# Side work of the mixers in small jobs let in by weight pieces on a credit, the output projection between queries and values of the next block's first pair, and longer norm gaps

## The chip, the cores and the metric

The kernel runs on one core of a Trainium2 chip. The metric is the device time of one execution in microseconds (us); before the change the median of three runs is 2594.67 us. Five engines work beside each other: PE (matmuls), DVE and ACT (elementwise work), POOL (here little more than clearing buffers) and SP (here the issue of DMAs). Each takes its own instructions in program order, and semaphores make one wait for another.

## The reference

One layer of a decoder trunk for 2048 tokens of width 1024, all in float32: a token mixer with three kinds of heads, then a gated MLP, each behind an RMS norm whose scale and shift come from a conditioning vector.

```python
c_act = jax.nn.silu(c)
mod = (c_act @ w_ada[l] + b_ada[l])[:, None, :]
sh1, sc1, g1, sh2, sc2, g2 = jnp.split(mod, 6, axis=-1)
h = rms_norm(x) * (1.0 + sc1) + sh1
x = x + g1 * token_mixer(h, w_in[l], ...)      # retention | HGRN2 | GLA, one output projection
h = rms_norm(x) * (1.0 + sc2) + sh2
x = x + g2 * conv_ffn(h, w_up[l], conv_w[l], conv_b[l], w_down[l])
return rms_norm(x) * final_gain
```

HGRN2 and GLA are recurrences with a decay for each key channel, `S_t = diag(exp(log_f_t)) S_{t-1} + k_t^T v_t`, `o_t = q_t S_t`, taken in chunks of 64 tokens; retention has a fixed decay for each head.

## The kernel before

Tokens lie along the free axis, in four blocks b = 0 to 3 of 512. A block goes through seven units, `ORDER` = h0, h1, g, h2, h3, r0, r1: four pairs of HGRN2 heads, all GLA heads, two pairs of retention heads. Names in the profile end in block and unit (qbh1_0: block 1, unit h0); the profile's groups leave the numbers out. A full-precision product is three matmuls of 128x512 on halves hi and lo of both factors (`split3`, L232 to L234).

**Weights.** `piece` (L213) and `tf512` (L274) fetch a weight in pieces of 512 KB: SP issues the load of the raw piece (r..., L220 or L282), ACT casts it to hi (h..., L221 or L285), and lo (l...) is computed by DVE in the first block, kept in DRAM, and reloaded from there later (L223, L290). There are two raw buffers and three each of hi and lo.

**A unit.** `unit_h` computes the forget gate (gemm pshf), the queries (pshq), and, for each second unit, the values and gates of the pair (psvg, four pieces in `tf512`). It then hands `gated` to a chain: seven levels, each of them four small matmuls (lv, L607), DVE scaling of queries and keys (L615, L617) and a masked copy (L629); then the keys' transposes (kT), the state update (u; S, L658), the output (o), its head norm (`post`, L542, L543) and, after a gap `POST_GAP`, the transposes to oT (L549, L552, L553). GLA and retention are alike.

**The order.** PE's order is written by hand. A `Clock` adds up the planned time of the matmuls that the projections issue (`adv`) and lets in steps of the chains when their time has come; `at(us, fn)` puts one in later, `until` runs them until a condition holds. The gaps count planned matmul time. The order of DVE, ACT and SP is made by a scheduler from the program order with priorities (`tc.high_priority`).

**Side work**, which no matmul of its own block waits for at once:
- conditioning rows, 48 in all: a load of 512 KB (wada, L190) and one DVE instruction (L197). Rows 16 to 47 run beside the mixers: the list `later` holds their numbers, and each weight piece takes one from it and runs it whole, load and use together.
- norm statistics of the next block (`norm1_stat`, L477): eight loads of x, squares on ACT, sums on DVE (san), then ssn and bcn on PE (`rstd`, L316 and L326) and Newton steps between them.
- the second half of the output projection of block b-1 (`out_finish`, L944): four pieces wo, eight outputs y, the residual (L937), the sums for the second norm (n2), and then `then`: eight rows of the normalised block, stored to h2d (L963 to L965). In block 0's case `then` waits in `put_off` until unit r0 of block 1 has been issued.
- sums of blocks of w_up and w_down for the MLP, in groups (`weight_sums_load` L884, `weight_sums` L892): two loads of 512 KB (wsd, wsu), four DVE additions (L896 to L899), two stores (L902). The main loop loads one or two groups ahead of a unit and sums them behind it. `early_sums` does a like thing with rows of h2d in block 3.

The loads of conditioning rows and sums share four buffers (xy). In the main loop `out_finish(b - 1)` stands behind unit h1 of block b, that is behind the pair's values; `norm1_stat` stands ahead of unit h3:

```python
            if i == len(ORDER) - 3 and b + 1 < NB:
                norm1_stat(b + 1)
...
            mk[kind](b, u, pos)
...
            if i == 1 and b:
                clock.until(lambda: None not in oTs[b - 1])
                out_finish(b - 1)
            for w in ws:
                weight_sums(*w)
```

Behind the mixers (from about 1310 us) the MLP runs; the change doesn't touch it.

Of the kernel before, what the change touches and what calls it, by code (L numbers as in the profile page):

```python
# [3 lines left out]

# [9 lines left out]
AF = mybir.ActivationFunctionType  # L14
# [34 lines left out]

M512, M256, MF = 0.227, 0.12, 0.224  # L50
LEVEL_GAP = (3.2, 4.8)
POST_GAP = 12.0


class Clock:
# [45 lines left out]
def trunk(ctx, tc, xT, vecs, cvec, cst, rope, msk, wada, win, walow, wgla, wout, wup, wdown, out):  # L101
# [91 lines left out]
    def ada(m, raw=None):  # L193

        if raw is None:
            raw = ada_load(m, False)
        V.tensor_tensor_reduce(raw[:], raw[:], c_act[:], 1.0, bada1[:, m:m + 1], op0=ALU.mult, op1=ALU.add,  # L197
                               accum_out=mod[:, m:m + 1])
# [30 lines left out]

    def split3(ps, lhs, rhs, first, last, more=False):  # L230
# [41 lines left out]
    def tf512(name, i, step=2):  # L272

        pss = [acc_ps(f"ps{name}_{c}") for c in range(NCH)]  # L274
        for q4 in range(4):
            half, sub = q4 // 2, q4 % 2
            src = win[i + half:i + half + step + 1:step][:, :, sub * 512:(sub + 1) * 512].rearrange("a p n -> p a n")
            if later:
                ada(later.pop(0))
            with tc.high_priority(offset=50):  # L280
                raw = pw.tile([P, 2, 512], F32, tag="wraw", name=f"r{name}_{q4}", bufs=NRAW)
                nc.sync.dma_start(raw[:], src)  # L282
                hi = pw.tile([P, 2, 512], F32R, tag="whi", name=f"h{name}_{q4}")
                lo = pw.tile([P, 2, 512], F32R, tag="wlo", name=f"l{name}_{q4}")
                S.copy(hi[:], raw[:])  # L285
                key = f"t{i}_{q4}l"
                flat = lo[:].rearrange("p a n -> p (a n)")
                one = [f"i{i + half + step * a}l" for a in range(2)]
                if key in kept:
                    nc.sync.dma_start(flat.bitcast(F32), kept[key][:])  # L290
# [40 lines left out]
    def sumsq(acc, x, k, name, sl=slice(0, TB), first=None):  # L331
        if k == 0 if first is None else first:
            S.activation(acc[:, sl], x[:, sl], AF.Square)
        else:
            sq = late(f"sq{name}{k}")
            S.activation(sq[:, sl], x[:, sl], AF.Square)
            V.tensor_tensor(acc[:, sl], acc[:, sl], sq[:, sl], op=ALU.add)

    def new_acc(name):
        return px.tile([P, TB], F32, tag="ssacc", name="sa" + name, bufs=1)  # L340
# [134 lines left out]
        return W  # L475

    def norm1_stat(b):  # L477
        acc = new_acc(f"n1_{b}")
        for k in range(KD):
            x = tmp(f"x{b}_{k}")  # L480
            nc.sync.dma_start(x[:], xT[b, :, k, :])
            sumsq(acc, x, k, f"n1_{b}_")
        bc1[b] = new_bc1(b)
# [99 lines left out]
    def gated(name, b, ui, pos, kq, decay, subs, qk, sel):  # L583
# [104 lines left out]
    def unit_h(b, u, pos):  # L688
# [122 lines left out]
    def retention(nm, b, r, pos, a, kk, kc, q, vsg):  # L811
# [54 lines left out]
            post(o, sg, nm)  # L866
        adv(12 * MF)
        yield None
        yield POST_GAP
        transposed(b, pos, o, nm)  # L870
        adv(4 * MF)

# [69 lines left out]
    put_off = []  # L942

    def out_finish(b, after_pieces=None, begun=None):  # L944


        acc = new_acc(f"n2_{b}")
        out_half(b, 1, acc, after_pieces, begun)
        rows = list(x1)
        bc = px.tile([P, TB], F32, tag="bc2", name=f"bc2_{b}", bufs=1)  # L950

        for m in range(KD if b == 0 else 0):
            nc.sync.dma_start(x1d[b, m][:], rows[m])

        def then():
            with tc.high_priority(offset=HOT if 0 < b < NB - 1 else -100):
                for m in range(KD):
                    t = rows[m] if b == NB - 1 else tmp(f"t2_{b}_{m}")[:]
                    if b == 0:
                        nc.sync.dma_start(t, x1d[b, m][:])  # L960
                    else:
                        nc.sync.dma_start(x1d[b, m][:], rows[m])
                    V.scalar_tensor_tensor(t, rows[m] if b else t, SC2[:, m:m + 1], bc[:], op0=ALU.mult, op1=ALU.mult)  # L963
                    S.activation(t, t, AF.Identity, bias=SH2[:, m:m + 1])
                    nc.sync.dma_start(h2d[b, m][:], t)  # L965
            done.add(("n2", b))
        clock.at(4.0 if b < NB - 1 else 5.5,
                 rstd(acc, f"n2_{b}", bc[:], then if b else lambda: put_off.append(then), gap=6.5))


    nth = {"w4": 0}
# [90 lines left out]
    gla_weights()  # L1062
    for hi, lo, raw, i in W0.values():
        keep(f"i{i}l", lo[:])
    jobs = [job for k in range(NF // 2) for job in (("d", k), ("u", 2 * k + 1))] + [("u", 0)]
    for b in range(NB):
        pos = 0
        for i, (kind, u) in enumerate(ORDER):
            if i == len(ORDER) - 3 and b + 1 < NB:
                norm1_stat(b + 1)  # L1070
            if b == 0 and i == 2:
                later += range(16, 24)
            if b == 1 and i == 1:
                later += range(24, 40)
            ws, es = [], None
            if b and i >= (3 if b == 1 else 1):
                ws = [weight_sums_load(*jobs.pop(0)) for _ in range(2 if b == 2 or (b, i) == (NB - 1, 5) else 1)]
            if b == NB - 1 and 1 <= i <= 4:
                es = early_sums_load(i - 1)
            mk[kind](b, u, pos)  # L1080
            pos += 2 if kind == "g" else 1
            if b == 1 and i == 5:
                assert not later
                later += range(40, 48)
                clock.until(lambda: put_off)
                put_off.pop()()
            if i == 1 and b:
                clock.until(lambda: None not in oTs[b - 1])
                out_finish(b - 1)
            for w in ws:  # L1090
                weight_sums(*w)
            if es:
                early_sums(*es)
# [481 lines left out]
```

## Time and profile before

| | |
|---|---|
| runs | 2594.67 us median of 3 (2591.9 to 2595.21) |
| profiled execution | 2594.2 us, span 2592.4 us |
| PE busy | 2495.8 us (96%) |
| DVE, ACT, POOL busy | 1993.2 us (77%), 1138.3 us (44%), 160.3 us (6%) |
| mean granted clock of PE | 0.987 |
| chain that ended last | PE 76%, DVE 12%, DMA 6%, issue 3% |

The span is the time from the first to the last instruction. Busy times are sums of an engine's instructions; the chain is followed back from the last instruction to whatever released each one. The mixers' four blocks take the time to about 1310 us; from there to the end the MLP keeps PE busy with little left over (561.58 of the 563 us from 1310 to 1873).

### The profile page before, as it was taken

To read this page: it belongs to the slowest core of one execution; us is meant where nothing else is said; L and a number is where in the kernel's file an instruction comes from. 1 tells how busy PE (TensorE), PEld (TensorE's weight loads), DVE (VectorE), ACT (ScalarE), POOL (GpSimd) and SP (SyncE) were. 2 spreads that over 40 slices of the span, in tenths; PEclk is the share of its full clock that TensorE was granted. 3 is DMA by queue.
4 is the path that set the end of the run, shared out by engine and by line. 5 is a ranking of instruction groups with operands and counts; after the bars stand their busy time and mean duration, and the time that the engine had idled before them with its cause. 6 is when DMAs were issued, how large, how long until landed. Compare 5 with 4: busy or idle time off the path is not lost.

```text
span 2592.4 us, 35722 instructions
## 1 busy us (share of the span) xinstructions
PE 2495.8 (96%) x12418; PEld 2098.8 (81%) x12418; DVE 1993.2 (77%) x3654; ACT 1138.3 (44%) x1946; POOL 160.3 (6%) x287
## 2 busy tenths in 40 slices
PE   5999999999998999999999999999999999999998
PEld 4888887888876888788878888888877888888887
DVE  8877878878677776776788888886777777778666
ACT  3333333334343343433465445555444545455542
POOL 1000000000000000000010000000001100100000
PEclk9999999999999999999999999999999999999999
DMA  8653538866478855787664454478676454447763
GB/s 307 216 160 123 172 121 299 306 200 212 161 262 305 282 165 163 282 291 239 201 212 157 151 168 148 145 226 284 202 240 183 141 158 145 139 150 230 232 193 133
DMA packets 233028, 525.05 MB, mean 203 GB/s; under 512 B 25456, under 2 KB 28560, under 8 KB 232848
## 3 DMA queue, kind: packets, MB, share of 16 engines
q1 hardware_dynamic: 229648, 512.28, 60.0%
q0 software_dynamic: 3200, 10.49, 1.1%
q8 instruction: 98, 1.61, 0.3%
q14 instruction: 82, 0.67, 0.1%
HBM read 397.37 MB, written 125.30 MB: 202 GB/s over the span
## 4 chain that ended last, share of the span: by engine, by line
PE 76%; DVE 12%; DMA 6%; issue 3%; ACT 1%; SPq 0%; DVEq 0%; ACTq 0%; POOL 0%; POOLq 0%
PE X L232 6%; PE X L234 6%; PE X L233 6%; PE Z L233 3%; PE Z L234 3%; PE lvh L607 3%; PE Z L232 3%; PE dX L233 3%; PE dX L232 3%; PE dX L234 3%; PE psvgh L232 2%; PE psvgh L233 2%; PE psvgh L234 2%; PE psqkvgr L232 2%; PE psqkvgr L234 2%
## 5 line engine op out<-in xcount | busy, mean ns | idle before, releaser
L232 PE MATMUL X<-B,A 128*128 128x512 f32 x572 | 224.1, 392 | 1.5 <-ACT u L1282 1.5
L233 PE MATMUL X<-B,A 128*128 128x512 f32 x572 | 223.5, 391 | 0.0
L234 PE MATMUL X<-B,A 128*128 128x512 f32 x572 | 223.3, 390 | 0.0
L998 DVE TENSOR_TENSOR dA<-rd,dA 128x512 fp32r<-128x512 f32 x154 | 106.1, 689 | 89.4 <-ACT dA L997 89.2
L997 ACT CAST dA<-rd 128x512 fp32r<-128x512 f32 x154 | 95.6, 621 | 141.1 <-PE dY L234 43.4
L998 DVE TENSOR_TENSOR A<-s,A 128x512 fp32r<-128x512 f32 x176 | 120.5, 686 | 40.9 <-ACT A L997 40.7
L232 PE MATMUL dX<-dB,dA 128*128 128x512 f32 x352 | 136.9, 389 | 0.0
L233 PE MATMUL dX<-dB,dA 128*128 128x512 f32 x352 | 136.9, 389 | 0.0
L234 PE MATMUL dX<-dB,dA 128*128 128x512 f32 x352 | 136.9, 389 | 0.0
L997 ACT CAST A<-s 128x512 fp32r<-128x512 f32 x176 | 108.7, 618 | 64.2 <-PE Z L234 45.2
L232 PEld LDWEIGHTS X<-B,A 128*128 128x128 f32 x572 | 107.9, 189 | 25.2 <-ACT u L1282 2.8
L234 PEld LDWEIGHTS X<-B,A 128*128 128x128 f32 x572 | 107.9, 189 | 22.4
L233 PEld LDWEIGHTS X<-B,A 128*128 128x128 f32 x572 | 108.0, 189 | 22.4
L607 PEld LDWEIGHTS lvh<-qbh,kh 128*128 128x128 f32 x896 | 116.8, 191 | 11.3 <-issue 3.5
L233 PE MATMUL Z<-B,A 128*128 128x512 f32 x308 | 120.4, 391 | 3.6 <-DVE B L998 3.6
L607 PE MATMUL lvh<-qbh,kh 128*128 128x128 f32 x896 | 120.8, 277 | 2.6 <-DVE kh L617 2.6
L234 PE MATMUL Z<-B,A 128*128 128x512 f32 x308 | 120.1, 390 | 0.0
L232 PE MATMUL Z<-B,A 128*128 128x512 f32 x308 | 119.9, 389 | 0.0
L998 DVE TENSOR_TENSOR dB<-rb,dB 128x512 fp32r<-128x512 f32 x154 | 105.5, 686 | 8.5 <-ACT dB L997 8.5
L998 DVE TENSOR_TENSOR A<-r,A 128x512 fp32r<-128x512 f32 x130 | 89.3, 687 | 28.5 <-ACT A L997 28.5
L232 PE MATMUL psvgh<-hvgh,ha 128*128 128x512 f32 (+1 forms) x256 | 103.1, 403 | 7.0 <-DVE sqh L702 3.7
L232 PE MATMUL psqkvgr<-hqkvgr,ha 128*128 128x512 f32 x256 | 106.2, 415 | 2.4 <-DVE sgh L530 1.7
(461 smaller groups left out, 7015.8 us busy)
## 6 DMA issues: line engine op xcount, KB each, us to landing
gs<-yv SPq DMA_DIRECT2D x154, 256.0 KB, 2.9
rb<-gs SPq DMA_DIRECT2D x154, 256.0 KB, 4.1
r<-wup SPq DMA_DIRECT2D x140, 256.0 KB, 3.5
s<-sumsu SPq DMA_DIRECT2D x136, 256.0 KB, 3.2
wada<-wada SPq DMA_DIRECT2D x48, 512.0 KB, 6.0
rd<-sumsd SPq DMA_DIRECT2D x88, 256.0 KB, 4.1
rd<-wdown SPq DMA_DIRECT2D x66, 256.0 KB, 3.9
x<-xT SPq DMA_DIRECT2D x64, 256.0 KB, 5.4
```

The lines of the kernel that those rows point to most:

```text
L232: T.matmul(ps, lhs[0], rhs[0], start=first, stop=False, skip_group_check=more)
L233: T.matmul(ps, lhs[0], rhs[1], start=False, stop=False, skip_group_check=more)
L234: T.matmul(ps, lhs[1], rhs[0], start=False, stop=last, skip_group_check=more)
L607: T.matmul(ps[:, c * P:(c + 1) * P].rearrange("p (h n s) -> p h n s", h=2, s=s), kq[:, c * P:(c + 1) * P], rhs, start=True, stop=True)
L997: S.copy(hi, src)
L998: V.tensor_tensor(lo, src, hi, op=ALU.subtract)
```

## The change

All instructions stay, in the same number on every engine; their order changes. Line numbers differ between the two kernels: L232 to L234 become L254 to L256, L607 becomes L637, and so on.

- A queue of jobs takes the place of `later`, `put_off` and the loads ahead of a unit. A job has a cost, a start (its load) and an end (its use). Behind each weight piece `tick` adds 1.8 to a credit, at most to 3.0, and starts jobs from the queue's head as far as it reaches; the end of each job runs when the next one has been started. What is left at a block's end is run there.
- `out_finish(b - 1)` moves into unit h1 of block b, between the queries' gemm and the pair's values.
- `POST_GAP` goes from 12 to 16 (in block 0 it was 15 for HGRN2 and GLA; retention in the last block keeps 12). The gap between ssn and bcn goes from 6.5 to 8.0, and the waits ahead of ssn from 22 to 5 and from 4 to 5.
- Norm statistics start one unit earlier; conditioning rows 24 to 31 move into block 0, and the groups of sums move from 4, 12, 7 to 6, 10, 7 in blocks 1, 2, 3.

```diff
-POST_GAP = 12.0
+POST_GAP, LAST_GAP = 16.0, 12.0
+JOB_RATE = 1.8
...
-    later = []
+    jobs, half_done, credit = deque(), [], [0.0]
+
+    def finish_jobs():
+        while half_done:
+            half_done.pop()()
+
+    def tick():
+        credit[0] = min(credit[0] + JOB_RATE, 3.0) if jobs else 0.0
+        if half_done and not jobs:
+            finish_jobs()
+        while jobs and jobs[0][0] <= credit[0]:
+            cost, start, end = jobs.popleft()
+            credit[0] -= cost
+            r = start()
+            finish_jobs()
+            half_done.append(lambda r=r, end=end: end(r))
+
+    def cond_jobs(ms):
+        for m in ms:
+            jobs.append((1.36, lambda m=m: ada_load(m, False), lambda raw, m=m: ada(m, raw)))
...
     def piece(src, name, key, ahead=50):
-        if later:
-            ada(later.pop(0))
...
+        tick()
         return hi, lo
...
-        clock.at(22.0, rstd(acc, f"n1_{b}", bc1[b][:], lambda: done.add(("n1", b)), gap=6.5))
...
+        def add(x, k):
+            sumsq(acc[0], x, k, f"n1_{b}_")
+            if k == KD - 1:
+                bc1[b] = new_bc1(b)
+                clock.at(5.0, rstd(acc[0], f"n1_{b}", bc1[b][:], lambda: done.add(("n1", b)), gap=8.0))
+        for k in range(KD):
+            jobs.append((0.7, lambda k=k: load(k), lambda x, k=k: add(x, k)))
...
-            yield 3.0 if i else POST_GAP + 3.0 if b == 0 else POST_GAP
+            yield 3.0 if i else POST_GAP
...
+        if between:
+            between()
         if u % 2:
             pss = tf512("vg" + nm, 4 * u - 2, 4)
...
+            for m in range(KD):
+                jobs.append((0.75, lambda m=m: row_load(m), lambda xt, m=m: row(xt, m)))
+        clock.at(5.0, rstd(acc, f"n2_{b}", bc[:], then, gap=8.0 if b < NB - 1 else 6.5))
...
+            jobs.append((2.7, lambda w=w: weight_sums_load(*w), lambda r: weight_sums(*r)))
...
+            if (b, i) == (0, 1):
+                cond_jobs(range(16, 24))
+            if b + 1 < NB and i == 3:
                 norm1_stat(b + 1)
...
+            if (b, i) == (0, 5):
+                cond_jobs(range(24, 32))
+            if (b, i) == (1, 2):
+                cond_jobs(range(40, 48))
+            if b and i >= 5:
+                take_sums({1: 3, 2: 5, 3: 2}[b])
+            if (b, i) == (NB - 1, 3):
+                take_sums(3)
+                for k in range(4):
+                    jobs.append((2.7, lambda k=k: early_sums_load(k), lambda r: early_sums(*r)))
+            if kind == "h" and u == 1 and b:
+
+                def between():
+                    clock.until(lambda: None not in oTs[b - 1])
+                    if b == 1:
+                        cond_jobs(range(32, 40))
+                    out_finish(b - 1)
+                unit_h(b, u, pos, between)
...
+        while jobs:
+            credit[0] = 3.0
+            tick()
+        finish_jobs()
```

What this does to the order, at three places. First SP in the third block, around the pieces of GLA's values (rvgg2_2 and rvgg2_3 are raw pieces, lvgg2 the reloaded low halves, h2d1 the normalised rows of block 1, wsd and wsu loads for sums, sumsd and sumsu their stores). Before:

```order
L282 DMA rvgg2_2_6939<-win 128x2x512
L290 DMA lvgg2_1_6904<-keptt18_1l_1251 128x1024
...
L290 DMA lvgg2_2_6942<-keptt18_2l_1302 128x1024
L902 DMA sumsd2_6596<-wsd2_1_5995 128x1024
L902 DMA sumsd2_6596<-wsd2_0_5994 128x1024
L902 DMA sumsu5_6603<-wsu5_1_5999 128x1024
L902 DMA sumsu5_6603<-wsu5_0_5998 128x1024
L890 DMA wsd3_0_6606<-wdown 128x1024
L890 DMA wsd3_1_6607<-wdown 128x1024
L890 DMA wsu7_0_6610<-wup 128x1024
L890 DMA wsu7_1_6611<-wup 128x1024
L282 DMA rvgg2_3_6995<-win 128x2x512
```

(Twelve more side transfers stand where the rows are left out: eight stores of h2d1 and four loads.) And in the changed kernel, all of them:

```order
L302 DMA rvgg2_2_6867<-win 128x2x512
L922 DMA wsd3_0_7713<-wdown 128x1024
L996 DMA h2d1_1_164<-t2_1_1_6472 128x512
L996 DMA h2d1_2_165<-t2_1_2_6618 128x512
L996 DMA h2d1_3_166<-t2_1_3_6623 128x512
L922 DMA wsd3_1_7714<-wdown 128x1024
L996 DMA h2d1_4_167<-t2_1_4_6668 128x512
L996 DMA h2d1_5_168<-t2_1_5_6673 128x512
L922 DMA wsu7_0_7826<-wup 128x1024
L310 DMA lvgg2_1_6829<-keptt18_1l_1262 128x1024
L302 DMA rvgg2_3_6979<-win 128x2x512
```

The stores of sums moved away from between the two raw pieces, and so did the loads behind them.

Second, PE in the second block, behind the queries of unit h1 (pshqh1_1): lvh1_0 are levels of unit h0, oTr0_1 the transposes of the last unit of block 0, psvgh1_1 the pair's values, y0_1 outputs of the projection. Before:

```order
L607 MATMUL lvh1_0_4_3281<-qbh1_0_3130,kh1_0_2967 128x128 x4
L232 MATMUL pshqh1_1_3254<-ha1_6_2678,hhqh1_1_3248 128x512
...
L549 MATMUL oTr0_1_3295<-c_all_86,or0_1_3186 128x128 x4
L232 MATMUL psvgh1_1_0_3322<-hvgh1_1_0_3331,ha1_0_2642 128x512
L233 MATMUL psvgh1_1_0_3322<-lvgh1_1_0_3332,ha1_0_2642 128x512
...
L607 MATMUL lvh1_0_8_3342<-qbh1_0_3130,kh1_0_2967 128x128 x4
```

(Left out are five matmuls of pshqh1_1, and four of psvgh1_1.) And in the changed kernel:

```order
L637 MATMUL lvh1_0_4_3302<-qbh1_0_3154,kh1_0_2991 128x128 x4
L254 MATMUL pshqh1_1_3272<-ha1_7_2708,hhqh1_1_3266 128x512
L255 MATMUL pshqh1_1_3272<-ha1_7_2708,hhqh1_1_3266 128x512
L256 MATMUL pshqh1_1_3272<-ha1_7_2708,lhqh1_1_3267 128x512
L637 MATMUL lvh1_0_8_3332<-qbh1_0_3154,kh1_0_2991 128x128 x4
L579 MATMUL oTr0_1_3340<-c_all_86,or0_1_3202 128x128 x4
L254 MATMUL y0_1_0_3359<-oTh0_2_0_2756,hwo0_1_0_3349 128x512
L255 MATMUL y0_1_0_3359<-oTh0_2_0_2756,hwo0_1_0_3349 128x512
```

Between the two levels stand three large matmuls instead of twelve, and behind the transposes come the outputs that use them.

Third, DVE in the first block, behind level 8 of GLA (lvg0_8): qbg and kg are its queries and keys, san1_1 the norm statistics of block 1, sqh0_3 the queries of unit h3. Before:

```order
L615 TENSOR_TENSOR qbg0_0_1126<-qbg0_0_1126,eg0_966 128x64x8
L615 TENSOR_TENSOR qbg0_1_1135<-qbg0_1_1135,eg0_966 128x64x8
L617 TENSOR_TENSOR kg0_964<-kg0_964,eg0_966 128x32x8
L629 COPY_PREDICATED atg0_0_1538<-m_all_87,lvg0_8_1791 128x64x8
L629 COPY_PREDICATED atg0_1_1540<-m_all_87,lvg0_8_1796 128x64x8
L337 TENSOR_TENSOR san1_1_1601<-san1_1_1601,sqn1_1_5_1627 128x512
L698 TENSOR_SCALAR kh0_3_1641<-snh0_3_1693,oml_89 128x512
L337 TENSOR_TENSOR san1_1_1601<-san1_1_1601,sqn1_1_6_1632 128x512
L702 TENSOR_TENSOR sqh0_3_1754<-pshqh0_3_1706,sqh0_3_1754 128x512
L337 TENSOR_TENSOR san1_1_1601<-san1_1_1601,sqn1_1_7_1637 128x512
```

And in the changed kernel:

```order
L645 TENSOR_TENSOR qbg0_0_1140<-qbg0_0_1140,eg0_980 128x64x8
L659 COPY_PREDICATED atg0_0_1559<-m_all_87,lvg0_8_1791 128x64x8
L645 TENSOR_TENSOR qbg0_1_1149<-qbg0_1_1149,eg0_980 128x64x8
L647 TENSOR_TENSOR kg0_978<-kg0_978,eg0_980 128x32x8
L659 COPY_PREDICATED atg0_1_1561<-m_all_87,lvg0_8_1796 128x64x8
L732 TENSOR_TENSOR sqh0_3_1750<-pshqh0_3_1702,sqh0_3_1750 128x512
L358 TENSOR_TENSOR san1_1_1437<-san1_1_1437,sqn1_1_7_1781 128x512
```

Two sums and kh moved ahead of the level; the last sum, which ssn1_1 on PE waits for, stands behind it in both.

More of the change, by code (lines that the diff above doesn't have):

```diff
@@ L2 @@
 import math
+from collections import deque
 from contextlib import ExitStack
@@ L686, in trunk, with unit_h @@
     tokens, waiting = set(), {}
-    def unit_h(b, u, pos):
+    def unit_h(b, u, pos, between=None):
         nm = f"h{b}_{u}"
@@ L868, in retention @@
         yield None
-        yield POST_GAP
+        yield POST_GAP if b < NB - 1 else LAST_GAP
         transposed(b, pos, o, nm)
@@ L953, in out_finish, with row_load, row @@
             nc.sync.dma_start(x1d[b, m][:], rows[m])
-        def then():
[L956 to L968, printed above, removed]
+        def row_load(m):
+            if b:
+                nc.sync.dma_start(x1d[b, m][:], rows[m])
+                return rows[m], rows[m] if b == NB - 1 else tmp(f"t2_{b}_{m}")[:]
+            t = tmp(f"t2_{b}_{m}")[:]
+            nc.sync.dma_start(t, x1d[b, m][:])
+            return t, t
+        def row(xt, m):
+            x, t = xt
+            V.scalar_tensor_tensor(t, x, SC2[:, m:m + 1], bc[:], op0=ALU.mult, op1=ALU.mult)
+            S.activation(t, t, AF.Identity, bias=SH2[:, m:m + 1])
+            nc.sync.dma_start(h2d[b, m][:], t)
+            if m == KD - 1:
+                done.add(("n2", b))
+        def then():
+            if b == NB - 1:
+                with tc.high_priority(offset=-100):
+                    for m in range(KD):
+                        row(row_load(m), m)
+                return
+            for m in range(KD):
+                jobs.append((0.75, lambda m=m: row_load(m), lambda xt, m=m: row(xt, m)))
+        clock.at(5.0, rstd(acc, f"n2_{b}", bc[:], then, gap=8.0 if b < NB - 1 else 6.5))
     nth = {"w4": 0}
@@ L1064, in trunk, with take_sums @@
         keep(f"i{i}l", lo[:])
-    jobs = [job for k in range(NF // 2) for job in (("d", k), ("u", 2 * k + 1))] + [("u", 0)]
+    sum_jobs = [job for k in range(NF // 2) for job in (("d", k), ("u", 2 * k + 1))] + [("u", 0)]
+    def take_sums(n):
+        for _ in range(min(n, len(sum_jobs))):
+            w = sum_jobs.pop(0)
+            jobs.append((2.7, lambda w=w: weight_sums_load(*w), lambda r: weight_sums(*r)))
     for b in range(NB):
@@ L1068, in trunk @@
         for i, (kind, u) in enumerate(ORDER):
-            if i == len(ORDER) - 3 and b + 1 < NB:
+            if (b, i) == (0, 1):
+                cond_jobs(range(16, 24))
+            if b + 1 < NB and i == 3:
                 norm1_stat(b + 1)
[L1071 to L1080, printed above, removed]
-            pos += 2 if kind == "g" else 1
[L1082 to L1093, printed above, removed]
+            if (b, i) == (0, 5):
[15 more added lines that the diff above has]
+                unit_h(b, u, pos, between)
+            else:
+                mk[kind](b, u, pos)
+            pos += 2 if kind == "g" else 1
+        while jobs:
+            credit[0] = 3.0
+            tick()
+        finish_jobs()
         if b + 1 < NB:
```

12 lines of the change are left out of this document (5 added, 7 removed).

## The prediction

> **What bounds the kernel now.** I read the table by stages first (windows of the four token blocks, as they pass through the mixers), then PE's waits, then the granted clock behind the long ones.
>
> ```profile
> core 0: us, PE busy (x) PEld busy (x) DVE busy (x) ACT busy (x) POOL busy (x), PEclk, DMA share, GB/s
> 60.00:300.00 240.00, 234.45 (x1343) 202.83 (x1342) 193.71 (x421) 86.77 (x176) 9.88 (x16) 0.98 0.52 171
> 300.00:630.00 330.00, 316.07 (x1774) 271.03 (x1773) 265.92 (x633) 130.06 (x248) 17.80 (x31) 0.99 0.68 228
> 630.00:955.00 325.00, 305.51 (x1682) 260.50 (x1681) 238.12 (x559) 122.34 (x234) 17.73 (x30) 0.98 0.69 235
> 955.00:1310.00 355.00, 342.54 (x1848) 291.18 (x1847) 253.50 (x571) 138.66 (x264) 19.05 (x34) 0.98 0.68 231
> ```
>
> In every stage of the mixers PE is the engine that works nearly all the time, with DVE at 71 to 81% beside it. So the program ends when PE has done its matmuls, and only PE's idle time can be won by another order: 5.55 + 13.93 + 19.49 + 12.46 = 51.4 us between 60 and 1310 us. The matmuls themselves are the same in number before and after. What the idle time consists of is in the waits:
>
> ```profile
> PE psvgg L232 <- ACT hvgg L285: 9.9, 2, 6.0
> PE pshqh L234 <- DMA lhqh<-kepti12l: 6.4, 1, 6.4
> PE oTh L549 <- DVE oh L543: 5.7, 4, 4.6
> PE bcn L326 <- DVE S L658: 5.3, 2, 2.6
> PE psvgh L232 <- DVE sqh L702: 3.7, 1, 3.7
> ...
> PE psvgh L232 <- ACT hvgh L285: 3.3, 2, 1.7
> ...
> PE lvh L607 <- DVE kh L617: 2.6, 3, 1.4
> ...
> PE uh L648 <- ACT kTh L637: 1.7, 1, 1.7
> ```
>
> (Total, times, longest.) A few long waits make most of it. The first is put down to ACT's cast of a weight piece, but ACT had been idle for 9.4 us when it came; the cast waited for the piece, and the piece for SP, which issues in order:
>
> ```profile
> 746.62 0.38 SPq L290 DMA_DIRECT2D lvgg<-keptt_2l  x1
> ...
> 757.60 1.26 SPq L890 DMA_DIRECT2D wsd<-wdown  x2
> 758.90 2.11 SPq L890 DMA_DIRECT2D wsu<-wup  x2
> 761.05 0.66 SPq L282 DMA_DIRECT2D rvgg<-win  x1
> ```
> ```profile
> 769.32 1.04 ACT L285 CAST hvgg<-rvgg 128x1024 fp32r<-128x1024 f32 x1 [9.38 <-DMA rvgg<-win]
> ```
>
> The piece was issued at 761.05, behind the loads of weight sums, and the cast began at 769.32. That is a queue held by side work.
>
> A second cost hangs on these waits. The granted clock just behind them (windows of PE alone: width, busy time, clock):
>
> ```profile
> 182.00:186.50 4.50, 3.75 (x12) 0.50 0.00 0
> 186.50:190.50 4.00, 4.00 (x14) 0.50 0.03 13
> ...
> 400.00:403.50 3.50, 3.50 (x15) 0.53 0.53 207
> ...
> 770.40:774.00 3.60, 3.58 (x9) 0.50 0.89 255
> 774.00:777.50 3.50, 3.50 (x22) 0.81 0.93 343
> 809.90:813.50 3.60, 3.51 (x10) 0.59 1.03 406
> ...
> 1091.00:1094.50 3.50, 3.48 (x8) 0.50 0.98 308
> 1094.50:1098.00 3.50, 3.50 (x22) 0.76 1.02 403
> ```
> ```profile
> 511.80:515.30 3.50, 3.50 (x12) 0.60 0.59 229
> 838.20:841.70 3.50, 3.50 (x19) 1.00 0.55 180
> ```
>
> All five stalls of 3.7 us or more are followed by 3.5 to 8 us at about half clock. Of the two stalls on S, 2.6 us each, one is (511.8), one isn't (838.2). The loss is busy time times (1 - clock): 1.9 + 2.0 + 1.7 + 1.8 + 0.7 + 1.4 + 1.7 + 0.8 for the five, 1.4 for the one on S: 13.4 us.
>
> **The change part by part, against the profiled execution's 2594.2 us** (span 2592.4; the median of the runs, 2594.67, lies 0.5 us above, which I leave out).
>
> *Jobs let in one by one.* In the order on SP above, between rvgg2_2 and rvgg2_3 stood 20 side transfers, among them four stores that wait for DVE's sums and four loads that wait for those stores; now eight stand there, none of them a store of sums. Followed through their conditions in the third and fourth block, each weight transfer there waits last for its own buffer, not for a job. So the two waits on hvgg (9.9), the one on lhqh (6.4) and the two on hvgh (3.3) go: 19.6 us. The wait on kTh (1.7) was ACT's, at the burst of normalised rows in the second block, and goes with the burst.
>
> *Longer gap ahead of transposes.* At 399.54 PE waited 4.6 us for oh. Block 1's gap goes from 12 to 16 us of planned matmuls, and the output projection no longer lies beside that chain: 4.6 goes.
>
> *Norm reductions moved.* The broadcast bcn stands behind ug in before, so its slot waits for the state updates S; in after it stands ahead of ug, with 8 us planned behind the sums. 5.3 goes. In the first block the wait on sqh (3.7) goes too: ssn1_1 stands nine matmuls behind the level matmul lvg0_8 where it stood eighteen behind, and so becomes the next to wait. What DVE does there took, in before:
>
> ```profile
> 177.69 1.28 DVE L615 TENSOR_TENSOR qbg<-qbg,eg 128x512 f32<-128x512 f32 x2
> ...
> 182.02 0.68 DVE L702 TENSOR_TENSOR sqh<-pshqh,sqh 128x512 f32<-128x512 f32 x1
> ```
>
> From 177.69 to the end of sqh are 5.0 us, with two sums and kh between that no longer stand there (about 0.6 each by the distance of their neighbours), and one sum added behind: about 4.0. PE does nine matmuls at 0.23, 2.1. With DVE level with PE the wait is 1.9, with the 1.7 us by which it lagged in before, 3.6. I take **2.6** (1.6 to 3.6).
>
> Removed: 19.6 + 1.7 + 4.6 + 5.3 + 3.7 = **34.9** of idle time and **13.4** of slow clock, 48.3 us.
>
> *Output projection ahead of the first pair's values.* It moves by one gemm on PE; the same DMAs and DVE sums go with it, past four value pieces on SP. Three places are new.
> (1) Levels lvh1_0_4 and lvh1_0_8 have three matmuls between them (0.7 us). DVE has to scale q and k there:
>
> ```profile
> L629 DVE COPY_PREDICATED ath<-m_all,lvh 128x512 f32<-128x512 uint32 x80 | 76.0, 950 | 0.0
> L615 DVE TENSOR_TENSOR qbh<-qbh,eh 128x512 f32<-128x512 f32 x96 | 65.9, 686 | 45.0 <-PE lvh L607 44.4
> ...
> L197 DVE CUSTOM_DVE_ANT_0 wada<-wada,c_act,vec 128x1024 f32<-128x1024 f32 x32 | 40.7, 1280 | 10.1 <-DMA wada<-wada 10.1
> ...
> L617 DVE TENSOR_TENSOR kh<-kh,eh 128x256 f32<-128x256 f32 x96 | 40.1, 418 | 0.0
> ...
> L896 DVE TENSOR_TENSOR wsu<-wsu 128x512 f32<-128x512 f32 x12 | 8.3, 691 | 5.7 <-DMA wsu<-wup 5.7
> ```
>
> 0.69 + 0.42 against 0.7 leaves 0.4; a half-finished norm of r0_1 ahead of them makes it more. **1.2** (0.5 to 2.5).
> (2) oTr0_1 now stands just ahead of y0_1_0, whose last slice needs it. How long that takes:
>
> ```profile
> 348.84 0.60 PE L549 MATMUL oTr<-c_all,or 128*128 128x128 f32 x4
> ```
> ```profile
> 351.09 0.74 DVE L553 SCALAR_TENSOR_TENSOR oTr<-oTr,vec,oTr 128x512 fp32r<-128x512 f32 x1
> ```
>
> 3.0 us from transposes to the low half; PE has the transposes and ten matmuls, 2.6. **0.4** (0 to 1.5).
> (3) Conditioning rows 32 to 39 load beside this projection through shared buffers, each load behind the use of an earlier one, and rvgh1_1_2 stands on SP behind row 37's load. The time from issue to landing, over the 48 rows' loads:
>
> ```profile
> DMA to landing us min/median/max: 3.3/6.0/10.4
> ```
>
> With landings of 6.0 the chain of three reuses ends some 3.4 us late for ssn2_0 and the piece, by my count along it; with landings between 3.3 and 4.5 it is in time. **1.5** (0 to 5.5).
>
> *The rest of the spread.* The same 1.28 us rows and groups of four 0.69 us sums now fall beside level chains that had none. Places that I didn't walk will show new small waits, as the places between the bursts do now: 51.4 - 34.9 = 16.5 us. These stay in kind; on top I add two thirds as much again, **11** (0 to 22), nearer to the upper end since all four blocks are reshuffled. The rate, the credit and the removed list cost nothing by themselves: they are of the build, and no instruction is added.
>
> Sum: 2594.2 - 48.3 + 2.6 + 1.2 + 0.4 + 1.5 + 11 = 2562.6, so **2563 us**.
>
> The Trainium skill, "TensorE: Matmul & The Clock Gate", Part 1, says that the array's clock falls to half after an idle window of about 3.4 us and returns after as long a busy one, the windows running freely. The trace agrees for the five long stalls, and 511.8 against 838.2 shows a stall of 2.6 us on either side of it. By that rule one stall costs about 1.7 us, the five 8.5 instead of 12 us, and the time would be about 2566 us, an estimate from that page. It also speaks against the change in one point: a new stall of 3 us or more, as at ssn1_1, could bring a slow stretch of its own.
>
> **Rivals.**
> *Nothing new is paid beside the four places.* No allowance, and these at their low ends (2.1): 2594.2 - 48.3 + 2.1 = 2548. For it: the gaps are longer everywhere. Against it: DVE is as loaded as before.
> *Weights are still held on SP.* A job's load waits for a buffer that a slower job holds, and the next piece waits behind it. Then 19.6 of idle time and 6.5 of clock (770 to 777, 810 to 813, 1091 to 1098) come back: 2563 + 26 = 2589. For it: row 37's load in front of rvgh1_1_2 is such a place. Against it: no whole group stands between two pieces any more.
> *Slower: the level chains become DVE's.* A level gives PE 15 to 18 matmuls, 3.4 to 4.1 us, and DVE 0.69 + 0.42 + 0.95 = 2.1; a group of sums takes 2.8, a row 1.3. Both in one level pass PE's time by one or two us, and PE waits at the next level. 23 groups and 32 rows of these stages are 63 + 41 = 104 us of DVE work. It decides from 42% of it uncovered, since 48.3 - 5.7 = 42.6 us are won elsewhere; at 60% the time is 2594.2 - 42.6 + 62 = 2614. Against it: DVE idles a fifth to a quarter of these stages, and in before the same work cost PE 2.6 us at kh.
>
> **How the numbers follow.** Forecast 0.70, nothing new paid 0.11, weights still held 0.11, DVE-bound 0.08. The range runs from the second's 2548 less a microsecond to 2584: the four places and the allowance at their upper ends (13.1 and 22) give 2581, and some of a held weight is possible with them. It holds 0.81. A measurement of this kernel tells about 0.2%, 5.2 us, from no change (its runs spread over 3.3); the held-weight case lies on that line and is halved. Faster 0.865, same 0.055, slower 0.08.
>
> **What would show it.** Right: no wait of PE above 4 us between 60 and 1310 us; hvgg, lhqh and hvgh gone from the waits; bcn no longer behind S; granted clock 0.99 in the mixers' stages, and idle time near 51.4 - 34.9 + 17 = 33 us. Wrong: a weight DMA still named by PE; waits on kh, sqh or san growing to tens of microseconds; new slow stretches of the clock; or time lost in the stages after 1310 us, which I take as unchanged.

## The result, and the profile after

The changed kernel takes 2553.27 us (median of 4, 2552.18 to 2560.24) against 2593.35 us before in the same series: a ratio of 0.9851, 95% interval 0.9831 to 0.987, some 40 us faster. The profiled execution took 2554.22 us, its span is 2552.4. The page's first lines:

```profile
span 2552.4 us, 35707 instructions
## 1 busy us (share of the span) xinstructions
PE 2480.7 (97%) x12418; PEld 2088.8 (82%) x12418; DVE 1986.5 (78%) x3654; ACT 1138.9 (45%) x1946; POOL 164.1 (6%) x287
```

These lines divide the gain. PE does the same 12418 matmuls in 2480.7 us where it took 2495.8, at a mean granted clock of 0.993 where it was 0.987: 15.1 us is less busy time. What the span has beside PE's busy time fell from 96.6 (2592.4 - 2495.8) to 71.7 us: 24.9 us is waiting that is gone. By stages, in the same stretches and columns as before:

```profile
60.00:300.00 240.00, 235.28 (x1353) 203.07 (x1352) 204.13 (x439) 87.89 (x175) 9.90 (x16) 0.99 0.57 190
300.00:630.00 330.00, 320.75 (x1794) 274.93 (x1793) 263.95 (x633) 131.14 (x249) 21.70 (x36) 0.99 0.68 228
630.00:955.00 325.00, 322.31 (x1799) 276.91 (x1799) 245.14 (x587) 128.48 (x246) 15.80 (x26) 1.00 0.69 233
955.00:1310.00 355.00, 345.78 (x1850) 293.09 (x1850) 263.12 (x580) 154.97 (x290) 24.98 (x41) 0.99 0.71 241
```

The third stretch, which held the two longest stalls, now has 2.7 us of idle time in place of 19.5, and 1799 matmuls in place of 1682. Over the four stretches PE is idle for 25.9 us, where it was 51.4. The changed kernel is ahead by then, so the last stretch holds more of the MLP. Cut at the MLP's first product X instead (window, width, PE's busy time, clock, DMA share, GB/s), before and after:

```profile
60.00:1270.70 1210.70, 1163.24 (x6491) 0.98 0.65 219
```
```profile
60.00:1233.00 1173.00, 1154.00 (x6487) 0.99 0.67 226
```

Up to X, PE is idle for 19.0 us instead of 47.5 and busy for 9.2 us less. The stretch from X to the end, nearly all of it the MLP, went from 1321.7 to 1319.4 us: 4.8 us less of busy time and 2.5 more of idle time. PE's waits (total, times, longest), those of the mixers and, on X, that of the MLP's first products:

```profile
PE psqkvgr L254 <- DVE orsg L160: 4.6, 2, 2.7
...
PE X L254 <- ACT hB L1037: 3.1, 1, 3.1
PE oTh L579 <- DVE oh L573: 3.0, 1, 3.0
...
PE psvgh L254 <- DVE sqh L732: 2.6, 1, 2.6
...
PE lvh L637 <- DVE kh L647: 2.0, 2, 1.6
...
PE ssn L337 <- DVE san L358: 1.2, 1, 1.2
PE og L593 <- DVE S L688: 1.1, 1, 1.1
...
PE y L255 <- DVE oTr L583: 1.0, 2, 0.7
...
PE psvgh L254 <- ACT hvgh L305: 0.4, 1, 0.4
```

No wait on a weight of the mixers is left but the last of these, 0.4 us, where there were 20. SP's queue at the piece that made the wait of 6.0 us on hvgg shows why (start, duration; SPq is SP's queue):

```profile
722.80 0.38 SPq L302 DMA_DIRECT2D rvgg<-win  x1
723.70 1.77 SPq L934 DMA_DIRECT2D sumsd<-wsd  x2
```
```profile
739.60 1.05 ACT L305 CAST hvgg<-rvgg 128x1024 fp32r<-128x1024 f32 x1
```

The last piece of GLA's values is issued at 722.80 and cast at 739.60, 16.8 us later, with ACT busy ahead of it from 729.09 on; no load of a raw GLA piece took more than 8.0 us to land. The piece waits for ACT and not ACT for the piece. Before, it left at 761.05, and ACT stood idle for 9.4 us. The clock behind the waits that are left (columns as in the cut at X):

```profile
170.10:173.50 3.40, 3.40 (x11) 0.51 0.55 172
183.70:187.10 3.40, 3.40 (x10) 0.50 0.00 0
316.80:320.20 3.40, 3.40 (x11) 0.50 0.32 94
497.70:501.10 3.40, 3.40 (x18) 0.50 0.79 300
1132.60:1136.00 3.40, 3.40 (x11) 0.50 0.64 246
1276.00:1279.40 3.40, 3.21 (x7) 0.50 0.32 95
```

Slow stretches remain in the mixers and at the MLP's start, each of 3.4 us at half clock, behind waits of 1.2 to 3.1 us.

### The profile page after: what moved, and what is told of

It reads as the page before. It is cut to its first block, busy times and chain, and to the rows that moved or that the text cites. A ratio compares the mean times of both kernels' runs of the same rounds, so it can differ in the third digit from the quotient of the medians.

```text
span 2552.4 us, 35707 instructions
## 1 busy us (share of the span) xinstructions
PE 2480.7 (97%) x12418; PEld 2088.8 (82%) x12418; DVE 1986.5 (78%) x3654; ACT 1138.9 (45%) x1946; POOL 164.1 (6%) x287
## 4 chain that ended last, share of the span: by engine, by line
PE 82%; DVE 8%; DMA 5%; issue 1%; ACT 1%; SPq 0%; DVEq 0%; POOL 0%; ACTq 0%; POOLq 0%
PE X L254 6%; PE X L256 6%; PE X L255 6%; PE lvh L637 3%; PE Z L255 3%; PE Z L256 3%; PE Z L254 3%; PE dX L254 3%; PE dX L255 3%; PE dX L256 3%; PE psqkvgr L254 2%; PE psqkvgr L256 2%; PE psqkvgr L255 2%; PE dY L254 2%; PE dY L256 2%; PE dY L255 2%
## 5 line engine op out<-in xcount | busy, mean ns | idle before, releaser
L254 PE MATMUL X<-B,A 128*128 128x512 f32 x572 | 223.4, 391 | 1.4 <-ACT u L1332 1.4
L256 PE MATMUL X<-B,A 128*128 128x512 f32 x572 | 222.8, 390 | 0.0
L254 PE MATMUL dX<-dB,dA 128*128 128x512 f32 x352 | 136.9, 389 | 0.0
L256 PE MATMUL dX<-dB,dA 128*128 128x512 f32 x352 | 136.9, 389 | 0.0
L254 PEld LDWEIGHTS X<-B,A 128*128 128x128 f32 x572 | 107.7, 188 | 24.4 <-ACT u L1332 2.2
L256 PEld LDWEIGHTS X<-B,A 128*128 128x128 f32 x572 | 107.5, 188 | 22.4
L637 PEld LDWEIGHTS lvh<-qbh,kh 128*128 128x128 f32 x896 | 116.3, 191 | 10.7 <-issue 3.5
L637 PE MATMUL lvh<-qbh,kh 128*128 128x128 f32 x896 | 120.5, 277 | 2.1 <-DVE kh L647 2.0
L254 PE MATMUL Z<-B,A 128*128 128x512 f32 x308 | 119.9, 389 | 0.0
L256 PE MATMUL Z<-B,A 128*128 128x512 f32 x308 | 119.8, 389 | 0.0
L254 PE MATMUL psqkvgr<-hqkvgr,ha 128*128 128x512 f32 x256 | 106.6, 416 | 4.6 <-DVE orsg L160 4.6
L1037 ACT CAST A<-r 128x512 fp32r<-128x512 f32 x130 | 81.0, 623 | 61.6 <-PE Z L256 59.4
```

The source lines that it names most:

```text
L254: T.matmul(ps, lhs[0], rhs[0], start=first, stop=False, skip_group_check=more)
L256: T.matmul(ps, lhs[1], rhs[0], start=False, stop=last, skip_group_check=more)
L637: T.matmul(ps[:, c * P:(c + 1) * P].rearrange("p (h n s) -> p h n s", h=2, s=s), kq[:, c * P:(c + 1) * P], rhs, start=True, stop=True)
L1037: S.copy(hi, src)
```

## The experiments

Times are medians; each ratio is to runs of the kernel before on the same chip.

| run | us | ratio | 95% interval |
|---|---|---|---|
| the change | 2553.3 | 0.9851 | 0.9831 to 0.9870 |
| a_jobsonly | 2567.0 | 0.9892 | 0.9873 to 0.9910 |
| a_gaps | 2555.7 | 0.9857 | 0.9827 to 0.9886 |
| a_nomove | 2565.2 | 0.9887 | 0.9865 to 0.9910 |
| a_burst | 2563.8 | 0.9880 | 0.9857 to 0.9902 |
| b_move | 2573.3 | 0.9915 | 0.9901 to 0.9928 |
| b_gaps | 2593.8 | 1.0002 | 0.9992 to 1.0012 |
| b_pool | 2631.6 | 1.0145 | 1.0131 to 1.0158 |
| b_warm | 2592.5 | 0.9996 | 0.9987 to 1.0006 |
| b_late | 2577.7 | 0.9939 | 0.9924 to 0.9954 |
| b_move_late | 2577.2 | 0.9939 | 0.9925 to 0.9953 |
| x_gap0 | 2566.8 | 0.9896 | 0.9881 to 0.9911 |
| x_rate | 2555.6 | 0.9853 | 0.9837 to 0.9869 |

### The three parts, one taken out or one left alone

**a_jobsonly**: the two edits of a_gaps and a_nomove below together.

> The changed kernel with the old gaps and with the output projection behind unit h1 again: of the three parts only the job queue is left. Theory (the bursts on SP made the long weight waits, and each long wait brought a slow stretch of the clock): the waits on hvgg, lhqh and hvgh are gone, 19.6 us of idle time and 6.5 of slow clock, and kTh with them; about 2565 us, between 2558 and 2572. Rival (the gain is made by the move and the gaps): 2580 us or more.

2567.0, as the theory had it, and hvgg, lhqh, hvgh and kTh are gone. Its longest waits in the mixers:

```profile
PE oTh L579 <- DVE oh L573: 8.8, 5, 4.6
PE pshfh L254 <- DVE sgg L560: 6.3, 3, 3.5
PE psqkvgr L254 <- ACT hqkvgr L305: 4.0, 1, 4.0
```

So a weight cast that cost nothing before, of a retention unit (hqkvgr), costs 4.0 us here. **a_gaps**:

```diff
-POST_GAP, LAST_GAP = 16.0, 12.0
+POST_GAP, LAST_GAP = 12.0, 12.0
-            yield 3.0 if i else POST_GAP
+            yield 3.0 if i else POST_GAP + 3.0 if b == 0 else POST_GAP
...
-... lambda: done.add(("n1", b)), gap=8.0))
+... lambda: done.add(("n1", b)), gap=6.5))
-        clock.at(5.0, rstd(acc, f"n2_{b}", bc[:], then, gap=8.0 if b < NB - 1 else 6.5))
+        clock.at(4.0 if b < NB - 1 else 5.5, rstd(acc, f"n2_{b}", bc[:], then, gap=6.5))
```

> The changed kernel with the old gaps (POST_GAP 12, 15 in the first block; 6.5 between ssn and bcn; 4 ahead of ssn of n2). Theory: the longer gaps are worth the wait on oh in the second block (4.6 us with 1.7 of slow clock) and something of bcn: about 2560 us, 2556 to 2565. Rival (the gaps are worth nothing once the jobs are spread): within 3 us of 2553.

2555.7: 2.5 us from the change, within what the intervals can't tell apart. (Its profiled execution, 2568.6 us, is the slowest of four; the others took 2554.1 to 2556.6.) **a_nomove**:

```diff
-                unit_h(b, u, pos, between)
+                unit_h(b, u, pos)
+                between()
```

> The changed kernel with the output projection behind unit h1 again, gaps and jobs as changed. Theory: the move costs the waits at lvh1_0_8 and oTr0_1 (2.3 us) and gives back no more than as much: 2550 to 2557 us. Rival (the move carries a main share of the gain): 2563 us or more.

2565.2, so the theory missed: with the jobs in place the move is still worth some 12 us. Its waits beside those of the changed kernel:

```profile
PE oTh L579 <- DVE oh L573: 5.6, 2, 3.0
PE psqkvgr L254 <- ACT hqkvgr L305: 3.9, 1, 3.9
PE pshfh L254 <- DVE sgg L560: 3.8, 2, 2.3
...
PE pshfh L254 <- ACT sgg L559: 2.7, 1, 2.7
```

sgg is the gate of GLA's values. Side work now falls on DVE and ACT beside GLA's values: four additions of a group of sums stand on DVE just ahead of the gates in the second and the fourth block (from 451.62 and 1062.82 us), a normalised row on DVE and ACT in the third (from 760.09). PE waits for the evacuation of these values (6.5 us), for oh once more (2.6) and for one weight cast (3.9). With the projection one gemm earlier the waits on sgg and on this cast are gone. In the profiled executions, of which a_nomove's (2561.7) is the fastest of its four, 7.5 us lie between the two kernels. **b_move** and **b_gaps** give the kernel before one part each. The gaps are those of the change's diff, with `clock.at(22.0` left as it was; the move alone is

```diff
+            if kind == "h" and u == 1 and b:
+
+                def between():
+                    clock.until(lambda: None not in oTs[b - 1])
+                    out_finish(b - 1)
+                unit_h(b, u, pos, between)
+            else:
+                mk[kind](b, u, pos)
...
-            if i == 1 and b:
-                clock.until(lambda: None not in oTs[b - 1])
-                out_finish(b - 1)
```

> The kernel before with the output projection moved between the queries and the values of the first pair, and nothing else of the change. Theory: the weight waits of the bursts stay; a few us either way, 2585 to 2600 us. Rival (the move is a main part of the gain): 2580 us or less.

> The kernel before with the longer gaps alone (POST_GAP 16, 8.0 between ssn and bcn, 5 ahead of ssn of n2; 22 ahead of ssn of n1 stays). Theory: the wait on oh (4.6 us, 1.7 of slow clock) goes, perhaps that of bcn (5.3, 1.4): 2581 to 2590 us. Rival: the longer gaps do nothing in the old order: within 3 us of before.

The gaps alone do nothing (1.0002): the wait on oh falls from 5.7 to 2.6 us in all, but two of 3.1 us each come up at GLA's queries (lvg on qbg, psvgg on qg). The move alone gives 20 us: again the rival was right. The first of its waits in the mixers:

```profile
PE psqkvgr L232 <- DVE orsg L158: 5.3, 2, 2.7
PE bcn L326 <- DVE S L658: 5.3, 2, 2.7
```

hvgg, lhqh and hvgh are gone though not one transfer was spread. The burst itself is still there. SP's queue in the third block of b_move, at the first and the second piece of GLA's values:

```profile
702.00 0.38 SPq L282 DMA_DIRECT2D rvgg<-win  x1
...
731.96 0.44 SPq L282 DMA_DIRECT2D rvgg<-win  x1
```

Between them stand the eight stores of normalised rows, four stores of sums and eight loads for sums, 30 us in all. In the kernel before they stood between the third and the fourth piece. Here PE comes to the pieces late enough: all four casts of hvgg follow without an idle gap of ACT.

### What holds the weights

**a_burst** replaces `min(credit[0] + JOB_RATE, 3.0)` by `credit[0] + 1e6`; **b_late** keeps the sums of the last two blocks away from GLA's values (and thereby moves four of the third block's twelve groups into the second):

```diff
-            if b and i >= (3 if b == 1 else 1):
-                ws = [weight_sums_load(*jobs.pop(0)) for _ in range(2 if b == 2 or (b, i) == (NB - 1, 5) else 1)]
+            if b and i >= 3:
+                ws = [weight_sums_load(*jobs.pop(0)) for _ in range(1 if (b, i) == (NB - 1, 6) else 2)]
```

**b_move_late** is this together with b_move.

> The changed kernel with an unlimited credit: the next weight piece starts all waiting jobs at once, in the same places of the program otherwise. Theory (it is the burst that holds the weights on SP): long waits on weight casts or weight DMAs return, with slow stretches of the clock behind those over 3.5 us; 10 to 40 us more than the changed kernel, about 2575 us. Rival (what counts is where the jobs are queued, not their rate): within 5 us of 2553.

> The kernel before, with the sums of the third and fourth block loaded from unit h2 on, two groups a unit (8 in each of the second and third block, 7 in the fourth, in place of 4, 12 and 7), so that none lies beside GLA's values any more. Theory (the stores of normalised rows and the sums' transfers, two bursts, meet on SP at GLA's values, and either out of the way frees the weights): the waits on hvgg go (9.9 us and 5.0 of slow clock) while lhqh (6.4), which lies in h3, stays or grows: about 2580 us, 2572 to 2588. Rival (the rows' stores alone, which have a high priority in these blocks, hold the weights): hvgg stays, within 5 us of 2594.

> The kernel before with both single edits that freed the weights: the output projection moved (2573 us alone) and the sums of blocks 3 and 4 kept to units h2 and later (2578 us alone); no job queue, old gaps. Theory (both take away the same waits, those on hvgg, lhqh and hvgh, so they don't add): 2566 to 2575 us, and the rest of the way to 2553 is the queue's spread of DVE work. Rival (they add): 2550 to 2560 us, and the queue itself is worth nothing.

a_burst is 10 us slower than the change, the low end of what was expected. Two waits on weights return, 7.6 us, and one of 2.3 on a low half that DVE makes:

```profile
PE psvgg L255 <- DMA lvgg<-keptt_0l: 4.7, 1, 4.7
...
PE psvgh L254 <- ACT hvgh L305: 2.9, 1, 2.9
```

The slow clock that was expected with them did not return: the profiled execution's mean clock is 0.994, and its 7.1 us over the change's are all waiting.

b_late came out as expected in time, and hvgg went; but lhqh went too, which was to stay. Of the weights only these and 0.2 us on lvgg are left:

```profile
PE psvgh L233 <- DMA lvgh<-keptt_0l: 2.2, 1, 2.2
...
PE psvgh L232 <- ACT hvgh L285: 1.9, 1, 1.9
```

So the stores of normalised rows, which b_late leaves where they were, don't hold a piece that PE waits for; at hvgg it took the sums' transfers beside them. But that the two have to meet is not shown. In b_move they still do, and it is only a piece that isn't needed soon that they hold. And lhqh stood behind other transfers, in the kernel before:

```profile
803.94 0.37 SPq L481 DMA_DIRECT2D x<-xT  x1
804.41 0.74 SPq L223 DMA_DIRECT2D lhqh<-kepti12l  x1
```

Ahead of it were the loads of x for the norm statistics and the last store of sums, and no store of rows; in b_move it left at 778.51, in b_late at 785.81. Why it leaves earlier there is not shown piece by piece. b_move_late bears out that the two gains are one: they would add to about 2557, and it took 2577.2, no better than either alone, and a little outside the expected range. Of that, 5 us are another wait: bcn behind S costs 10.3 us there, 5.3 in b_move. The queue of jobs takes the same waits away (a_jobsonly), which is why 0.9892 and 0.9915 don't multiply to 0.981 but to 0.9857 in a_gaps, where both are.

**b_pool** makes this edit for the loads and stores of sums, the loads for the early sums and the stores of rows and residual:

```diff
-            nc.sync.dma_start(t[:], src[2 * n + i])
+            nc.gpsimd.dma_start(t[:], src[2 * n + i])
```

> The kernel before, with the side transfers (loads and stores of sums, loads for the early sums, stores of the normalised rows and of the residual) issued on POOL's queue in place of SP's; all of DVE's and ACT's side work stays where it was, in bursts. Theory (weights were held on SP's queue): the waits on hvgg, lhqh and hvgh go, 19.6 us with 6.5 of slow clock: about 2568 us, 2562 to 2575. Rival (the burst of DVE work, or the load on the 16 DMA engines, made them): they stay, 2585 us or more.

It took 2631.6, slower by 1.45%, and neither theory had that. No long wait on a weight is left; PE waits for DVE, and DVE for the loads of sums:

```profile
PE lvg L607 <- DVE atg L629: 15.9, 6, 4.2
```
```profile
DVE wsu L896 <- DMA wsu<-wup: 34.5, 9, 6.6
...
DVE wsd L896 <- DMA wsd<-wdown: 21.5, 5, 8.5
```

DVE too works in order. Once the sums' loads stand behind held transfers on another queue, the additions stand waiting on DVE, and the level chains' copies behind them. What was held moved from SP to DVE. The run speaks for the mechanism, not for its price on SP, and how much of the loads' delay is POOL's own way of issuing stays open.

### The clock

**b_warm** adds matmuls that nobody reads, into an accumulator of their own, where PE waits in the kernel before (the numbers are how many):

```diff
+    def fill(name, n):
+        p = late_ps("fill" + name)
+        for _ in range(n):
+            T.matmul(p[:], h[0][:, 0, 0:P], h[0][:, 0, :], start=True, stop=True)
+
+    FILL = {("hqh2_3", 0): 26, ("vgg2", 3): 25, ("vgg3", 3): 16, ("vgh0_3", 0): 15}
```

> The kernel before, with 82 matmuls of 128x512 added that nobody reads, put where PE waited in four of the long stalls (15 ahead of the last quarter of psvgh0_3's first piece, 25 and 16 ahead of the last piece of psvgg2 and psvgg3, 26 ahead of pshqh2_3), each a little shorter than the stall. Theory (idle time of PE brings the slow clock): the granted clock stays at 1.0 there, and 8 to 10 us are saved although PE does 18.6 us more work: about 2584 us. Rival (the clock falls for another reason, or wakes no sooner): no gain, 2593 us or more.

No gain (0.9996). In the windows the theory is right at each of the four filled places and wrong about the sum. b_warm first, then the kernel before in the same places:

```profile
183.80:187.20 3.40, 3.40 (x21) 1.00 0.00 0
...
316.40:319.80 3.40, 3.40 (x18) 0.50 0.76 231
...
769.40:772.80 3.40, 3.40 (x20) 1.00 0.97 324
838.70:842.10 3.40, 3.40 (x10) 0.50 0.55 169
```
```profile
183.80:187.20 3.40, 3.40 (x14) 0.50 0.00 0
...
317.70:321.10 3.40, 2.67 (x15) 1.00 0.12 28
...
770.40:773.80 3.40, 3.38 (x8) 0.50 0.85 252
838.70:842.10 3.40, 3.40 (x20) 1.00 0.60 194
```

At 183.8 and 769.4 the clock stays whole. Followed matmul by matmul, b_warm is 3.6 us ahead at 191 us. Then it slows at 316.4, behind two waits of 1.4 and 0.7 us that cost nothing before, and again at 838.7 behind a wait of 2.6; and at 818 the wait for a weight is longer by 2.0 us, since PE comes to it 3.8 us sooner and the piece only 1.8. The lead is gone: X starts at 1271.1 us, 1270.7 before. The same instructions with the same waits run at half clock or not, as the stall happens to lie (more on this at the end).

### Two variants of the change

**x_gap0** has `POST_GAP + 4.0 if b == 0 else POST_GAP` ahead of HGRN2's and GLA's transposes; **x_rate** has `JOB_RATE = 1.4`.

> The changed kernel with a gap of 20 in place of 16 ahead of the transposes of HGRN2 and GLA in the first block. Theory: the wait of 3.0 us for oh at 169.6 us goes, and with it one or two slow stretches of the clock (1.7 each): 2548 to 2551 us. Rival (DVE is behind there, and the wait only moves to the next matmul that needs it): within 2 us of 2553.

> The changed kernel with a rate of 1.4 in place of 1.8 a weight piece; what is left at a block's end is run there at once. Theory: the rate is not critical between a burst and this: within 4 us of 2553. Rival (DVE's backlog beside the level chains is what is left of the waits): 2545 us or less.

x_rate is level with the change. x_gap0 removes the wait it was aimed at, and is slower by 13 us, which neither theory allowed for. Its profiled execution is the slowest of its four, 2570.66 us:

```profile
PE 2493.8 (97%) x12418; PEld 2099.3 (82%) x12418; DVE 1987.6 (77%) x3654; ACT 1137.1 (44%) x1946; POOL 164.5 (6%) x287
```

Against the change, PE is busy for 13.1 us longer and idle for only 3.4 longer. A gap in the first block moves everything that the hand-written clock puts in after it, in all four blocks, and other waits come up (3.6 us on nw, a step of a norm), but most of the loss here is the clock, 0.988 against 0.993. The other three executions had 0.990 and 0.991; how their time divides is not known. No variant beat the change.

## Why the prediction was right, point by point

The forecast was 2563 in a range of 2547 to 2584; 2553.3 is nearer to the case in which nothing new is paid (2548). The sum was to be 18.2 us less waiting and 13.4 us of clock, all of it in the mixers; over the whole program it was 24.9 and 15.1. In the mixers alone, up to X, it was 28.5 us less waiting, and 7.4 of clock.

- **Jobs let in one by one, 19.6 and 1.7**: shown. hvgg, lhqh and kTh are gone from the waits, hvgh is down to 0.4, and a_jobsonly has 28.9 us of gain without the other parts. That SP's queue held the pieces of hvgg is shown by b_late, with one correction: the stores of rows alone don't. That the transfers hold no weight once they stand on another queue is shown by b_pool. Nor is spreading them the only way to free the weights, as b_move shows.
- **Longer gap, 4.6**: the wait at h1_0's transposes is gone, but the gap was not needed for it. a_jobsonly, with gap and place as before, still has it at 4.6; with the longer gap and the old place (a_nomove, b_gaps) 2.6 stay; with the old gap and the new place (a_gaps) it is gone, though 4.1 us of a wait at ssn2_0 come up there.
- **Norm reductions, 5.3 and 3.7**: both went from their places, and bcn not for the 8 us behind the sums: with 6.5 (a_gaps) it doesn't wait for S either. 2.6 of a wait on sqh came up at another place.
- **The four priced places**: 2.6 + 1.2 + 0.4 + 1.5 = 5.7 forecast. ssn1_1 took 1.2, lvh1_0_8 1.6, the first use of oTr0_1 0.7, ssn2_0 nothing: 3.5. The chain of loads landed in time.
- **The move** was charged with its new waits and credited with nothing of its own. This is the step that was wrong. b_move and a_nomove show it worth 20 us alone and 12 beside the jobs. Much of its gain was in the forecast all the same, since the waits that it also removes were counted under the jobs; the waits on sgg (2.8), which grow when the jobs come without the move (6.3 in a_jobsonly), were left to the allowance as things that would stay.
- **The allowance, 11**: mis-sized. New waits at places not walked are 12.5 us (orsg 4.6, oh 3.0, sqh 2.6, S 1.1, smaller ones 1.2). But waits that I had counted as staying went too, 10.0 us (sgg 2.8, kh 2.2, sgh 1.7, oh 1.1, lvgh 0.8, smaller ones 1.4). The net is 2.5. With the four places and the 34.9 removed that is 28.9 us, close to the 28.5 up to X; the rest of the program has 3.5 us more idle time than before, among it the 3.1 us that X waits for hB.
- **The clock, 13.4**: that the whole program gave 15.1 is luck. In the mixers slow stretches took 15.9 us of busy time before and take 8.5 now, by the records of the clock: the long stalls' stretches went, as forecast, but five stretches are there behind waits of 1.2 to 3.0 us, and the sum had no term for them. 4.8 us of the 15.1 lie behind X, where the forecast counted no gain: a slow stretch of 10.2 us from 1307.8 before is one of 3.4 from 1276.0 now.

So the errors pulled against each other: the waiting came out 10 us better than forecast in the mixers, the clock there 6 us worse, and some 5 us of clock came from elsewhere. Of the signs named ahead, the longest wait is 3.1 us, hvgg and lhqh are gone, bcn no longer stands behind S, and the clock in the stages is 0.99 or better; idle time is 25.9 us where 33 was expected. One sign of being wrong came as well: new slow stretches, at 170.1 and 497.7 us for instance.

Of the rivals, held weights didn't come, nor did DVE become the bound: its waits at kh fell from 2.6 to 2.0 us. In the changed kernel's mixers each slow stretch is 3.4 us long and follows waits of 1.2 to 3.0 us. The Trainium skill, "TensorE: Matmul & The Clock Gate", Part 1, gives a window of about 3.4 us for the fall to half clock and for the return: the lengths agree, but the waits ahead of them are shorter than an idle window of that length.

## What to carry to other kernels

Where transfers share one in-order queue with the weights, look at which of them wait for a computation, and how soon the matmuls need the weight behind them. Here spreading the transfers gave 29 us, moving one group away 16, and moving work so that the same burst stood ahead of a piece needed later 20; these gains don't add. Moving transfers to another queue moves the waiting to whatever engine is in order behind them. When an order is written by a planned clock, a gain of half a per cent from one of its numbers says little about that number: here changes of one number moved the time between 2553 and 2567.

## What the runs showed of the hardware

In the mixers the granted clock falls to half in stretches of 3.4, 6.8 or 10.2 us, each beginning in or just behind a stall of PE. Within one profiled execution all of them start on one grid: those of the changed kernel, at 170.1, 183.7, 316.8, 497.7, 1132.6 and 1276.0 us, lie 4, 39, 53, 186 and 42 steps of 3.413 us apart. Whether a stall brings one depends on how it lies on that grid. Of the two stalls on S in the kernel before, 2.6 us each, the one at 509.1 lies in one step, and the next step, from 512.5, runs at half clock; the one at 835.6 is shared by two steps, with 1.2 and 1.4 us of idle time, and the clock stays whole:

```profile
509.13:512.54 3.41, 0.77 (x7) 0.99 0.93 305
833.34:836.76 3.42, 2.21 (x18) 1.00 1.04 400
836.76:840.17 3.41, 1.98 (x11) 1.00 0.61 247
```

1.4 and 0.7 us close together fall into one step in b_warm (313.0 to 316.4 us, followed by half clock) and into two in the kernel before (from 314.5). In all the profiled executions, from 60 to 1310 us, no step in which PE was idle for 2.0 us or more was without a slow step behind it, and the least idle time that began a slow stretch was 1.05 us; between the two both came. What decides there stays open.

Executions of one kernel differ: ten of b_gaps ran from 2589.9 us at a mean clock of 0.991 to 2602.88 at 0.987. That is 3.2 us for each thousandth of the clock, where a thousandth of the span is 2.6. The grid lies differently from one kernel's profiled execution to the next; that it does so between executions of one kernel, and makes this spread, would fit, but is not shown. A comparison over fewer runs than these can mistake the spread for an effect.
